# One level of a seven-product scheme in the second product of two MLPs, with weight sums made by DMA

## The chip, the core and the metric

The kernel runs on one core of a Trainium2 chip. The metric is the device time of one execution in microseconds (us); lower is better. The kernel before took 1751.53 us as the median of three runs (1750.19 to 1755.14).

## The reference, cut to what matters

Two transformer blocks run one after the other on x of 512 tokens by 1024 features, all in 32-bit floats. Each block has a mixer and an MLP with a hidden width of 4096; the first has a cross-attention over 256 memory rows between them. The part that is changed:

```python
def squared_relu_mlp(h, w1, w2):                 # first block: ffn_w1 (1024x4096), ffn_w2 (4096x1024)
    return jnp.square(jax.nn.relu(h @ w1)) @ w2
x = x + squared_relu_mlp(rmsnorm(x, norm_ffn[l]), ffn_w1[l], ffn_w2[l])
...
u = rmsnorm_2(x, norm_mlp_g[i]) @ w_up[i]        # second block: w_up_2, w_down_2, same sizes
x = x + jnp.square(jax.nn.relu(u)) @ w_down[i]
```

The first block's mixer (`hybrid_mixer`) holds a gated delta rule with 4 heads. The second block's mixer holds an mLSTM and a sliding-window attention.

## The kernel before, in words

x stays in SBUF with features on the 128 partitions: 8 tiles of 128 features by 512 tokens. A product with a weight is computed in three matmuls: both operands are split into a high part (a cast to float32r) and a low part (the rest, again float32r), and high*high, high*low and low*high are added in one PSUM bank (`mm3`, lines 227 to 229). A *granule* is 256 output features of a weight over 1024 inputs. It comes as two loads of 512 KB by SP's queue into `wr` (line 207, two buffers); ScalarE casts each to `wh` (line 210) and VectorE subtracts to get `wl` (line 211). Then TensorE does two output tiles with 8 x 3 = 24 matmuls of 512 columns each (`proj_fm`).

`ffn` cuts the hidden width into 4 quarters of 1024. `up(q)` makes one quarter of the hidden layer: VectorE takes max(.,0) times the token's norm from PSUM (line 805), ScalarE squares (806), and the result is split into high and low (256, 257). `down(q)` multiplies that quarter with 1024 rows of the second weight and adds the tiles into x (line 402). The order written is up 0, up 1, down 0, up 2, down 1, up 3, down 2, down 3; two sets of slots hold two quarters at a time.

The order on each engine's queue is not written out by hand: the framework records the operations with their dependencies and a scheduler puts each at a place in its engine's queue by estimated times. An operation whose inputs are there early can so be put far ahead of its place in the program text. On the chip every engine works through its queue in that fixed order; an instruction that waits holds all behind it on that engine. DMAs are issued by instructions in the queues of SP, ScalarE (ACT) and GpSimd (POOL), and a wait ahead of a DMA sits in that queue too.

The first mixer (0 to about 308 us) does projections, and for each of the 4 heads `dn_head`: GpSimd makes `slg` from a mask and the decay (line 536), TensorE multiplies it (513), ScalarE takes the exponential (539), GpSimd masks it (540), and all later steps of the head need it: VectorE makes `dM` from it (547), GpSimd masks that (568), and so on. GpSimd also scales the gating values (373, 374), gates each head's output (669) and adds squares for the norms (271).

## Time and profile before

| | |
|---|---|
| runs shown, median | 1751.53 us |
| the profiled execution's own time | 1754.69 us |
| its span, first to last instruction | 1752.9 us |
| TensorE busy / weight loads busy | 1722.4 us (98%) / 1431.2 us (82%) |
| VectorE / ScalarE / GpSimd busy | 1010.4 us (58%) / 722.1 us (41%) / 144.0 us (8%) |
| moved by DMA | 155.09 MB, 88 GB/s on average |
| first MLP, first to last product | about 458 to 818 us |

"Busy" is the time in which the profile shows an instruction on the engine. Matmuls are pipelined, so the time from one matmul's start to the next's is read from the timeline, not from the length shown for one. Idle time of an engine that nobody waits for costs nothing. "DMA share" is the mean busy share of the core's 16 DMA engines.

### The profile page before, as it was taken

The page shows a single profiled execution, that of the slowest core. Times are in us where ns is not written, and L with a number is a line of the kernel's source. Part 1 is how long each engine was busy: PE and PEld are TensorE (multiplying, and loading weights), DVE is VectorE, ACT ScalarE, POOL GpSimd, SP SyncE. Part 2 cuts the span into 40 slices and gives each one's busy share as a digit, 9 for nine tenths or more (in the row PEclk, how much of TensorE's full clock was granted, in tenths as well). Part 3 has the DMA queues.
Part 4 walks back from the last instruction along what each step waited for, and adds up shares of the span by engine and source line. Part 5 has one row for each costly group of instructions (what it writes and reads, how often), then busy time and mean ns, then how long its engine had stood idle before and what let it go on. Part 6 is the DMA issues. An engine that isn't in the chain of part 4 may idle for free.

```text
span 1752.9 us, 22699 instructions
## 1 busy us (share of the span) xinstructions
PE 1722.4 (98%) x8772; PEld 1431.2 (82%) x8772; DVE 1010.4 (58%) x2037; ACT 722.1 (41%) x1258; POOL 144.0 (8%) x123
## 2 busy tenths in 40 slices
PE   8999999999999999999999999999999999999998
PEld 7987788878888888888888887788888888888887
DVE  6998886655544434447756469865555434344455
ACT  5344544544432333334444447654234323232344
POOL 2212311201000000012000000000120000000101
PEclk9999998999999999999999999999999999999999
DMA  6322232312322223222222221223232223233221
GB/s 197 97 73 63 62 98 87 108 49 73 96 97 96 96 96 96 91 91 85 73 73 81 88 73 49 73 72 97 87 97 88 91 95 97 96 96 108 90 99 64
DMA packets 49676, 155.09 MB, mean 88 GB/s; under 512 B 9504, under 2 KB 10656, under 8 KB 49568
## 3 DMA queue, kind: packets, MB, share of 16 engines
q1 hardware_dynamic: 48848, 152.51, 27.3%
q8 instruction: 69, 1.13, 0.3%
q10 hardware_dynamic: 720, 1.13, 0.2%
q14 instruction: 39, 0.32, 0.1%
HBM read 151.26 MB, written 2.10 MB: 87 GB/s over the span
## 4 chain that ended last, share of the span: by engine, by line
PE 87%; DVE 9%; ACT 2%; issue 1%; DMA 0%; POOL 0%; SPq 0%; ACTq 0%; DVEq 0%
PE psd L228 26%; PE psd L229 26%; PE psd L227 25%; DVE wl L211 2%; PE c L564 1%; ACT wh L210 1%; PE c L513 1%; PE lg L1148 1%; PE po L1175 1%; DVE e L314 1%; PE m L1069 1%; DVE S L369 1%; PE c L229 0%; PE c L228 0%; PE c L227 0%
## 5 line engine op out<-in xcount | busy, mean ns | idle before, releaser
L229 PE MATMUL psd<-S,wl 128*128 128x512 f32 (+1 forms) x1936 | 759.4, 392 | 0.5 <-DVE wl L211 0.5
L227 PE MATMUL psd<-S,wh 128*128 128x512 f32 (+1 forms) x1936 | 757.0, 391 | 0.0
L228 PE MATMUL psd<-S,wh 128*128 128x512 f32 (+1 forms) x1872 | 735.0, 393 | 0.0
L211 DVE TENSOR_TENSOR wl<-wr,wh 128x1024 fp32r<-128x1024 f32 (+2 forms) x284 | 351.0, 1236 | 229.9 <-ACT wh L210 228.8
L210 ACT CAST wh<-wr 128x1024 fp32r<-128x1024 f32 (+2 forms) x284 | 292.5, 1030 | 436.5 <-PE psd L228 406.4
L227 PEld LDWEIGHTS psd<-S,wh 128*128 128x128 f32 x1936 | 365.9, 189 | 79.1 <-ACT S L256 0.4
L229 PEld LDWEIGHTS psd<-S,wl 128*128 128x128 f32 x1936 | 364.7, 188 | 76.7 <-DVE wl L211 1.1
L228 PEld LDWEIGHTS psd<-S,wh 128*128 128x128 f32 x1872 | 352.4, 188 | 74.6 <-DVE S L260 0.5
L271 POOL TENSOR_TENSOR acc<-acc,sq 128x512 f32<-128x512 f32 (+1 forms) x47 | 67.7, 1439 | 918.6 <-ACT sq L269 918.4
L402 DVE TENSOR_TENSOR x_fm<-psd,x_fm 128x512 f32<-128x512 f32 x88 | 60.7, 690 | 137.9 <-PE psd L229 137.8
L228 PE MATMUL psd<-wl,S 128*128 128x256 f32 (+2 forms) x480 | 137.5, 286 | 0.6 <-DVE wl L211 0.6
L229 PE MATMUL psd<-wh,S 128*128 128x256 f32 (+2 forms) x480 | 137.1, 286 | 0.0
L227 PE MATMUL psd<-wh,S 128*128 128x256 f32 (+2 forms) x480 | 136.7, 285 | 0.0
L805 DVE SCALAR_TENSOR_TENSOR e<-psd,bc 128x512 f32<-128x512 f32 x64 | 44.3, 692 | 112.3 <-PE psd L229 109.4
L806 ACT ACTIVATE e<-e 128x512 f32<-128x512 f32 x64 | 40.5, 633 | 135.1 <-DVE e L805 135.1
L228 PEld LDWEIGHTS psd<-wl,S 128*128 128x128 f32 x480 | 91.7, 191 | 1.4 <-DVE wl L211 1.0
L227 PEld LDWEIGHTS psd<-wh,S 128*128 128x128 f32 x480 | 91.8, 191 | 0.4
L229 PEld LDWEIGHTS psd<-wh,S 128*128 128x128 f32 x480 | 91.9, 191 | 0.1
L257 DVE TENSOR_TENSOR S<-e,S 128x512 fp32r<-128x512 f32 (+1 forms) x84 | 56.7, 675 | 49.3 <-ACT S L256 49.2
L256 ACT CAST S<-e 128x512 fp32r<-128x512 f32 (+1 forms) x84 | 50.5, 601 | 42.9 <-POOL e L932 27.1
L259 ACT ACTIVATE S<-x_fm,vec 128x512 fp32r<-128x512 f32 x40 | 28.9, 722 | 56.8 <-DVE x_fm L402 37.4
L314 DVE SCALAR_TENSOR_TENSOR e<-e,vec,e 128x511 f32<-128x511 f32 (+2 forms) x60 | 46.6, 779 | 2.6 <-ACT e L311 2.2
(418 smaller groups left out, 1523.0 us busy)
## 6 DMA issues: line engine op xcount, KB each, us to landing
wr<-in_ffn_w_dram SPq DMA_DIRECT2D x64, 512.0 KB
wr<-in_w_up_dram SPq DMA_DIRECT2D x32, 512.0 KB
wr<-in_w_down_dram SPq DMA_DIRECT2D x32, 512.0 KB
wr<-in_w_in_qk_dram SPq DMA_DIRECT2D x16, 512.0 KB
wr<-in_w_in_v_dram SPq DMA_DIRECT2D x12, 512.0 KB
wr<-in_xa_wk_dram SPq DMA_DIRECT2D x8, 512.0 KB
wr<-in_xa_wv_dram SPq DMA_DIRECT2D x8, 512.0 KB
wr<-in_xa_wq_dram SPq DMA_DIRECT2D x8, 512.0 KB
```

The costliest lines, as they stand in the source:

```text
L210: nc.scalar.copy(hi[:, c], raw[:, c])
L211: nc.vector.tensor_tensor(out=lo[:, c], in0=raw[:, c], in1=hi[:, c].bitcast(F32), op=ALU.subtract)
L227: mm(ps, ah, bh, start=first, stop=False)
L228: mm(ps, ah, bl, start=False, stop=False)
L229: mm(ps, al, bh, start=False, stop=last)
L256: nc.scalar.copy(hi, src)
L257: nc.vector.tensor_tensor(out=lo, in0=src, in1=hi.bitcast(F32), op=ALU.subtract)
L271: eng.tensor_tensor(out=acc, in0=acc, in1=sq, op=ALU.add)
L314: nc.vector.scalar_tensor_tensor(out=c[:, s:], in0=xr[:, :T - s], scalar=w(j), in1=c[:, s:], op0=ALU.mult, op1=ALU.add)
L402: self.nc.vector.tensor_tensor(out=self.x[:, o], in0=ps, in1=self.x[:, o], op=ALU.add)
L805: nc.vector.scalar_tensor_tensor(out=t, in0=ps, scalar=0.0, in1=bc, op0=ALU.max, op1=ALU.mult)
L806: nc.scalar.activation(t, t, AF.Square)
```

## The change

**The scheme.** In each MLP, for each quarter q and each granule of 256 outputs, the second product is 256 outputs x 1024 inputs times 1024 inputs x 512 tokens. The outputs, the inputs and the tokens are each cut into two halves. Instead of eight products of halves seven are done, of sums of halves (Strassen's scheme in Winograd's form). `st_gemm` does per granule 7 products of 4 x 3 = 12 matmuls with 256 columns, 84 in all, in place of 48 with 512 columns, and adds each finished PSUM value into a 128x256 part of x, 7 additions per granule; four of the seven products go on adding in a PSUM tile that has just been read (`more=True`).

**The operands of the hidden layer.** `st_fill` makes, per up granule, four sums and differences of halves (`ms`) on VectorE, and splits all seven operand parts into high and low. There is one set of slots; the order is now up 0, down 0, up 1, down 1, and so on.

**The weights.** The second weights are laid out so that one granule is four pieces of 128x512 per partition block (`halves`). Three of the seven weight operands are such pieces, four are sums of them. The sums stand in DRAM tiles, 1 MB for each of the 16 granules of each MLP. `sum_jobs` makes them with DMAs from DRAM to DRAM: per granule three copies issued on ScalarE's queue (4 pieces of 256 KB in all), then four DMAs on GpSimd's queue that add 256 KB each to what stands at the destination (`accum_op`); the third waits for the first, the fourth for the third. The program text calls one step of these jobs before each granule load (`job`): the first MLP's from the first mixer on, the second's from the first MLP on. `st_weights` then loads 7 pieces per granule (three loads of 512 KB, one of 256 KB), where two loads of 512 KB were before, and splits them. In the MLPs the loads rotate over five sets of buffers in place of two `wr` and three `wh`, `wl`.

**Slots.** To make room, slots are renumbered (`perm`), the pool `sp2`/`sp3` is dropped in the MLPs for `fp`, four PSUM banks go to `px`, the input `p` of the last stage is loaded ahead of the second MLP, and the work after the last addition into an x tile (`post`) is called for two tiles at the end of a granule.

**Order on GpSimd.** First head of the first mixer, GpSimd's queue. Before, between the scaling of the gating values (lines 373, 374) and the first head's masks:

```order
L373 TENSOR_TENSOR S_42_322<-S_42_322,S_41_321 128x256
L374 TENSOR_TENSOR S_42_322<-S_42_322,S_41_321 128x256
L536 TENSOR_TENSOR slg_1238<-masks,dg_1052 128x512
L540 TENSOR_TENSOR slg_1238<-slg_1238,masks 128x512
L568 TENSOR_TENSOR dT_1273<-dM_1258,masks 128x512
L536 TENSOR_TENSOR slg_1600<-masks,dg_1052 128x512
```

Now, from the last adding DMAs of the first MLP to the first head's second mask (line 584 was 536, 588 was 540, 616 was 568); the bracket names what the instruction waits for, where DMASW and DMAHW are completions of earlier DMAs from GpSimd and from SP or ScalarE:

```order
L584 TENSOR_TENSOR slg_1307<-masks,dg_1114 128x512 [waits DVE_49]
L219 DMA sums_ffn_w_14_77<-sums_ffn_w_14_77 128x512 [waits DMAHW5_49,DMASW0_49]
L219 DMA sums_ffn_w_15_78<-in_ffn_w_dram 128x512 [waits DMAHW2_49]
L219 DMA sums_ffn_w_14_77<-sums_ffn_w_14_77 128x512 [waits DMASW4_49,DMASW2_49]
L219 DMA sums_ffn_w_15_78<-in_ffn_w_dram 128x512 [waits DMAHW3_49]
...
L219 DMA sums_w_down_1_80<-in_w_down_dram 128x512 [waits DMAHW3_49]
L588 TENSOR_TENSOR slg_1307<-slg_1307,masks 128x512 [waits Activation_49]
L219 DMA sums_w_down_1_80<-sums_w_down_1_80 128x512 [waits DMASW7_49,DMASW5_49]
```

All 128 adding DMAs, those of the second MLP (`sums_w_down`) too, now stand in the first mixer's part of the queue: 58 ahead of the first head's first mask, 71 ahead of its second, and all 128 ahead of the last head's second mask (the fourth `L588`). Behind it no such DMA follows.

**Order on ScalarE.** Near the start of the first mixer, where the weights `w_in_gv` are cast (line 256 was 210). Before:

```order
L210 CAST wh_336<-wr_335 128x1024
L210 CAST wh_342<-wr_341 128x1024
L210 CAST wh_508<-wr_507 128x1024
```

Now:

```order
L256 CAST wh_373<-wr_372 128x1024 [waits DMAHW4_49,DVE_49,PE_49]
L216 DMA sums_ffn_w_1_64<-in_ffn_w_dram 256x1x512 [waits DMAHW2_49]
L256 CAST wh_379<-wr_378 128x1024 [waits DMAHW5_49,DVE_49,PE_49]
L217 DMA sums_ffn_w_1_64<-in_ffn_w_dram 128x512
L218 DMA sums_ffn_w_1_64<-in_ffn_w_dram 128x512
L216 DMA sums_ffn_w_2_65<-in_ffn_w_dram 256x1x512 [waits DMAHW7_49]
L217 DMA sums_ffn_w_2_65<-in_ffn_w_dram 128x512 [waits DMAHW0_49]
L218 DMA sums_ffn_w_2_65<-in_ffn_w_dram 128x512 [waits DMAHW1_49]
L256 CAST wh_550<-wr_549 128x1024 [waits DMAHW3_49,DVE_49,PE_49]
```

All 96 copies, those of the second MLP too, stand in the first mixer's part of ScalarE's queue; most wait for an earlier DMA. (The number in a bracket's name is no time.)

**Order on TensorE.** From the first MLP's first quarter of `up` to its `down` (`x_5077` and `x_5078` are PSUM tiles of the first granule, `psd_5079` its third; `S_...` the operand's parts). The scheduler does the first 9 matmuls of a product, leaves the last 3, which need the newest up tile, and goes on with another product:

```order
L277 MATMUL x_5078<-S_824_4772,wl_5061 128x256
L275 MATMUL psd_5079<-S_828_4776,whx_5054 128x256
...
L276 MATMUL psd_5079<-S_829_4777,whx_5054 128x256 [waits DVE_49]
L275 MATMUL x_5077<-S_826_4774,wh_5060 128x256 [waits DVE_49]
...
L277 MATMUL psd_5079<-S_828_4776,wlx_5055 128x256
L275 MATMUL x_5195<-S_830_4778,whx_5172 128x256
L276 MATMUL x_5195<-S_830_4778,whx_5172 128x256
L275 MATMUL x_5078<-S_824_4772,wh_5060 128x256 [waits Activation_49]
```

So 30 matmuls with 256 columns stand between the last `up` matmul and the first that needs the second half of the newest tile in its split form. In the kernel before a whole `up` quarter stood there.

The diff, cut to its core:

```diff
     def slot(self, i, shape, dt=F32):
+        i = self.perm[i]
         return (self.sp if i < 9 else self.sp2).tile(shape, dt, tag=f"S{i}", name=self.uid(f"S{i}"))
...
+    def sum_jobs(self, name):
+        nc, n = self.nc, 16
+        def step(i):
+            if i < n:
+                a, s = self.D[name][i], self.sums[name][i]
+                nc.scalar.dma_start(s[:, 1::2], a[:, 0:2])
+                nc.scalar.dma_start(s[:, 0:1], a[:, 2:3])
+                nc.scalar.dma_start(s[:, 2:3], a[:, 2:3])
+            acc = lambda o, i: nc.gpsimd.dma_start(o, i, accum_op=ALU.add)
+            if 0 <= i - 1 < n:
+                a, s = self.D[name][i - 1], self.sums[name][i - 1]
+                acc(s[:, 0:1], a[:, 3:4])
+                acc(s[:, 2:3], a[:, 0:1])
+            if 0 <= i - 2 < n:
+                s = self.sums[name][i - 2]
+                acc(s[:, 1:2], s[:, 0:1])
+            if 0 <= i - 3 < n:
+                s = self.sums[name][i - 3]
+                acc(s[:, 3:4], s[:, 1:2])
+        self.jobs += [(lambda i=i: step(i)) for i in range(n + 3)]
+    def job(self):
+        if self.jobs:
+            self.jobs.pop(0)()
+    def wtiles(self, kt, n):
+        p, b, x = self.wp, (2, 3), ""
+        if self.wx is not None:
+            self.wn = (self.wn + 1) % 5
+            if self.wn > 2:
+                p, b, x = self.wx, (2, 2), "x"
+        return (self.t(p, [P, kt, n], "wr" + x, bufs=b[0]), self.t(p, [P, kt, n], "wh" + x, F32R, bufs=b[1]),
+                self.t(p, [P, kt, n], "wl" + x, F32R, bufs=b[1]))
...
         nc = self.nc
-        raw = self.t(self.wp, [P, kt, n], "wr", bufs=2)
-        hi = self.t(self.wp, [P, kt, n], "wh", F32R)
-        lo = self.t(self.wp, [P, kt, n], "wl", F32R)
+        raw, hi, lo = self.wtiles(kt, n)
...
     def wgran(self, name, g, n=256, nk=8, pieces=None):
+        if self.wx is None:
+            self.job()
...
-    def mm3(self, ps, ah, al, bh, bl, first, last):
+    def mm3(self, ps, ah, al, bh, bl, first, last, more=False):
         mm = self.nc.tensor.matmul
-        mm(ps, ah, bh, start=first, stop=False)
-        mm(ps, ah, bl, start=False, stop=False)
-        mm(ps, al, bh, start=False, stop=last)
+        mm(ps, ah, bh, start=first, stop=False, skip_group_check=more)
...
-    def ffn(self, w1, w2, xh, xl, acc, evac):
...
-        rs = self.tok_rs(acc, "rs")
-        bc = self.tok_bc(rs, "bc")
-        H = {}
...
-        up(0)
-        up(1)
-        down(0, self.add_res)
-        up(2)
-        down(1, self.add_res)
-        up(3)
-        down(2, self.add_res)
-        down(3, evac)
...
+        ms = self.t(self.fp, [P, 4, 256], "ms", bufs=1)
+        TT(out=ms[:, 3], in0=e2[:, h[1]], in1=e1[:, h[1]], op=ALU.subtract)
+        TT(out=ms[:, 1], in0=e1[:, h[0]], in1=e1[:, h[1]], op=ALU.subtract)
+        STT(out=ms[:, 2], in0=ms[:, 3], scalar=-1.0, in1=e1[:, h[0]], op0=ALU.mult, op1=ALU.subtract)
+        STT(out=ms[:, 0], in0=ms[:, 2], scalar=-1.0, in1=e2[:, h[0]], op0=ALU.mult, op1=ALU.subtract)
+        self.split_sb(t[6][:, 0, k], t[6][:, 1, k], e1[:, h[0]])
+        self.split_sb(t[4][:, :, k], t[5][:, :, k], e2.rearrange("p (a c) -> p a c", a=2))
+        self.split_sb(t[2][:, :, k], t[3][:, :, k], ms[:, 2:4])
+        self.split_sb(t[0][:, :, k], t[1][:, :, k], ms[:, 0:2])
+    def st_weights(self, name, g):
+        a, s = self.D[name][g], self.sums[name][g]
+        out = []
+        for src in (a[:, 0:2], s[:, 0:2], s[:, 2:4], a[:, 3:4]):
+            hi, lo = self.wload(src, src.shape[1], T)
+            out.extend((hi[:, i], lo[:, i]) for i in range(src.shape[1]))
+        return [out[i] for i in (0, 2, 3, 1, 4, 5, 6)]
...
+    def st_gemm(self, name, g, H, o1, post):
+        nc = self.nc
+        TT = nc.vector.tensor_tensor
+        w = self.st_weights(name, g)
+        _, hi, lo = H
+        X, Z = (self.t(self.px, [P, T], "x")[:, :256] for _ in range(2))
+        Y = self.psd()[:, :256]
+        x = [[self.x[:, o1 + n, t * 256:t * 256 + 256] for t in range(2)] for n in range(2)]
+        def prod(i, ps, m, first):
+            ah, al = w[i]
+            for k in range(4):
+                c = slice(k * P, (k + 1) * P)
+                self.mm3(ps, ah[:, c], al[:, c], hi[m][:, k], lo[m][:, k], first and k == 0, k == 3, not first)
+        def add(n, t, ps, op=ALU.add):
+            TT(out=x[n][t], in0=x[n][t], in1=ps, op=op)
+        prod(0, X, 0, True)
+        add(0, 0, X)
+        prod(1, Z, 4, True)
+        add(1, 1, Z, ALU.subtract)
+        prod(2, X, 5, False)
+        add(0, 1, X)
+        prod(3, Y, 1, True)
+        add(0, 0, Y)
+        prod(4, X, 6, False)
+        add(1, 1, X, ALU.subtract)
+        prod(5, Z, 2, False)
+        add(0, 1, Z)
+        prod(6, X, 3, False)
+        add(1, 0, X, ALU.subtract)
+        for o in (o1, o1 + 1):
+            post(o)
+    def ffn(self, w1, w2, xh, xl, acc, slots, post):
+        nc = self.nc
+        with self.tc.tile_pool(name=self.uid("px"), bufs=4, space=PSUM) as self.px:
+            bc = None
+            for q in range(4):
+                H = None
+                for g in range(4):
+                    pss, es = [], []
+                    self.proj_fm(self.wgran(w1, 4 * q + g), xh, xl, (0, 1), lambda o, ps: pss.append(ps))
+                    self.job()
+                    if bc is None:
+                        bc = self.tok_bc(self.tok_rs(acc, "rs"), "bc")
+                    for ps in pss:
+                        e = self.t(self.fp, [P, T], "eh", bufs=4)
+                        nc.vector.scalar_tensor_tensor(out=e, in0=ps, scalar=0.0, in1=bc, op0=ALU.max, op1=ALU.mult)
+                        nc.scalar.activation(e, e, AF.Square)
+                        es.append(e)
+                    H = H or self.st_operand(slots)
+                    self.st_fill(H, g, *es)
+                for g in range(4):
+                    self.st_gemm(w2, 4 * q + g, H, 2 * g, post if q == 3 else lambda o: None)
...
         K = Kern(tc, ctx, D, out, dbg)
         K.setup()
+        K.sum_jobs("ffn_w2")
         K.mixer()
         mem = K.memory()
         with tc.tile_pool(name="sp2", bufs=1) as K.sp2:
             op = K.w_out1()
             op = K.xattn(*op, mem)
+        K.sum_jobs("w_down_2")
+        with tc.tile_pool(name="fp", bufs=1) as K.fp:
+            K.sp2 = K.wx = K.fp
             ev, fin = K.between()
-            K.ffn("ffn_w1", "ffn_w2", *op, ev)
+            K.ffn("ffn_w1", "ffn_w2", *op, (0, 1, 4, 7, 8, 9, 10), ev)
+            K.wx = None
             op2 = fin()
+        K.perm = [2, 3, 5, 6, 0, 1, 4, 7, 8]
         mh, ml = K.mixer2(*op2)
-        with tc.tile_pool(name="sp3", bufs=1) as K.sp2:
-            xh, xl = K.pair((9, 10)), K.pair((11, 12))
-            acc = K.new_acc()
-            def ev(o, ps):
-                K.nc.vector.scalar_tensor_tensor(out=K.x[:, o], in0=ps, scalar=0.5, in1=K.x[:, o], op0=ALU.mult, op1=ALU.add)
-                K.norm_tile(o, xh, xl, acc, "norm_mlp_g_2")
-            for g in range(4):
-                K.proj_fm(K.wgran("w_out_2", g), mh, ml, (2 * g, 2 * g + 1), ev)
-            K.dump("x5", K.x)
+        K.perm = list(range(13))
...
+def halves(w):
+    v = w.reshape(4, 2, P, -1, 2, P).transpose(3, 2, 4, 1, 0, 5).reshape(-1, P, 4, 4 * P)
+    return np.ascontiguousarray(v)
```

86 lines of the change are left out of this document (50 added, 36 removed).

## The prediction, made before the changed kernel was run

> **What bounds the kernel now.** I read the page's first part and its chain first.
>
> ```profile
> PE 1722.4 (98%) x8772; PEld 1431.2 (82%) x8772; DVE 1010.4 (58%) x2037; ACT 722.1 (41%) x1258; POOL 144.0 (8%) x123
> PE 87%; DVE 9%; ACT 2%; issue 1%; DMA 0%; POOL 0%; SPq 0%; ACTq 0%; DVEq 0%
> PE psd L228 26%; PE psd L229 26%; PE psd L227 25%; DVE wl L211 2%; PE c L564 1%; ACT wh L210 1%; PE c L513 1%; PE lg L1148 1%; PE po L1175 1%; DVE e L314 1%; PE m L1069 1%; DVE S L369 1%; PE c L229 0%; PE c L228 0%; PE c L227 0%
> ```
>
> TensorE's product matmuls are 77% of the chain; no DMA and no GpSimd work is on it. Next the busy times by stretch, for the first mixer (to about 308 us) and one stretch of the first MLP. Columns: stretch, its length, busy us of PE, PEld, DVE, ACT, POOL with their counts, clock, DMA share, GB/s.
>
> ```profile
> 0.00:44.00 44.00, 38.95 (x215) 33.74 (x216) 28.91 (x53) 24.40 (x40) 11.22 (x16) 1.00 0.60 196
> 44.00:88.00 44.00, 43.46 (x302) 39.94 (x302) 40.34 (x112) 16.80 (x25) 12.50 (x16) 1.00 0.31 97
> 88.00:132.00 44.00, 42.59 (x258) 36.89 (x257) 40.10 (x84) 20.94 (x52) 7.16 (x5) 1.00 0.22 73
> 132.00:176.00 44.00, 42.94 (x249) 34.99 (x248) 39.36 (x115) 17.43 (x42) 9.04 (x8) 1.00 0.20 63
> 176.00:220.00 44.00, 41.20 (x235) 33.93 (x234) 36.58 (x93) 22.71 (x64) 14.14 (x14) 0.92 0.22 63
> 220.00:264.00 44.00, 40.95 (x340) 38.84 (x339) 38.81 (x145) 21.06 (x54) 7.47 (x4) 1.00 0.33 97
> 264.00:308.00 44.00, 40.68 (x298) 38.78 (x297) 27.40 (x69) 18.30 (x41) 4.80 (x3) 0.88 0.32 95
> 458.00:548.00 90.00, 90.00 (x389) 1.00 0.29 94
> ```
>
> In the MLP TensorE has no gap at all, so fewer columns there are time won. The mixer is another case: TensorE is at 92 to 99% and VectorE, until 264 us, at 83 to 92%; the heads' chains run through GpSimd, and TensorE's gaps from 44 to 308 us are only 264 - 251.8 = 12 us. A head that comes late has little to hide behind.
>
> **The products.** The start of one matmul after another, 512 and 256 columns, from the timeline:
>
> ```profile
> 620.18 0.40 PE L227 MATMUL psd<-S,wh 128*128 128x512 f32 x1
> 631.32 0.39 PE L227 MATMUL psd<-S,wh 128*128 128x512 f32 x1
> 885.04 0.28 PE L227 MATMUL psd<-wh,S 128*128 128x256 f32 x1
> 889.94 0.28 PE L227 MATMUL psd<-wh,S 128*128 128x256 f32 x1
> ```
>
> 48 matmuls lie in the first 11.14 us (0.2321 each), 42 in the second 4.90 us (0.1167 each): half the columns, half the time, so short matmuls lose nothing here. A granule goes from 48 x 0.2321 = 11.14 to 84 x 0.1167 = 9.80 us; 32 granules win 42.8 us.
>
> What lies beside it in the MLP:
>
> ```profile
> L211 DVE TENSOR_TENSOR wl<-wr,wh 128x1024 fp32r<-128x1024 f32 x266 | 333.5, 1254 | 227.9 <-ACT wh L210 226.9
> L257 DVE TENSOR_TENSOR S<-e,S 128x512 fp32r<-128x512 f32 x76 | 53.4, 702 | 49.1 <-ACT S L256 49.1
> L256 ACT CAST S<-e 128x512 fp32r<-128x512 f32 x76 | 47.2, 621 | 35.2 <-POOL e L932 27.1 <-DVE e L395 6.2
> L805 DVE SCALAR_TENSOR_TENSOR e<-psd,bc 128x512 f32<-128x512 f32 x64 | 44.3, 692 | 112.3 <-PE psd L229 109.4 <-ACT bc L293 2.9
> L806 ACT ACTIVATE e<-e 128x512 f32<-128x512 f32 x64 | 40.5, 633 | 135.1 <-DVE e L805 135.1
> L710 DVE TENSOR_TENSOR e<-psd,bc x8: 404/419/425, 232.5 to 266.6; 128x256 f32<-128x256 f32 x8
> ```
>
> VectorE per up granule: two weight subtracts 2.5, two line-805 operations 1.4, four `ms` at 0.42 each 1.7, splits 0.42 + 3 x 0.70 = 2.5, together 8.1 of 11.1 us; per down granule 3.5 subtracts 4.4 and seven additions 2.9, together 7.3 of 9.8 us. That is 74%, where TensorE is full: hidden. Loads grow from 2.10 to 2.88 MB per pair of granules in 20.9 us, 138 GB/s at a share of about 0.43: hidden. From up to down the newest tile needs 0.69 + 0.63 + 0.62 + 0.70 = 2.6 us, 3.9 with one weight subtract ahead of it on VectorE, and TensorE has 30 x 0.1167 = 3.5 us of other matmuls; I take 1 us for each of 8 transitions, 8 us (nothing, up to 8 x 5.8 = 46 if no cover held and all `ms` and splits showed). The late `post` for two tiles costs about 3 us per MLP, 6 us. The MLPs together: -42.8 + 8 + 6 = **-29 us**.
>
> **The sums.** They are the other half of the matter. 32 granules x 4 pieces of 256 KiB are 33.55 MB copied and as much added, and the order puts all of it into the first mixer. What a DMA engine gives, from loads with the same 2 KB rows:
>
> ```profile
> x_fm<-in_x_dram SPq DMA_DIRECT2D x8, 256.0 KB
> wr<-in_w_in_u_dram SPq DMA_DIRECT2D x8, 256.0 KB
> 4.00:8.00 4.00, 3.30 (x15) 2.75 (x15) 1.91 (x6) 2.62 (x5) 0.00 (x0) 1.00 0.95 296
> 24.00:28.00 4.00, 4.00 (x19) 3.29 (x18) 1.21 (x1) 2.04 (x2) 0.33 (x1) 1.00 0.92 331
> ```
>
> 296 GB/s at 0.95 is 312 GB/s at full share (360 in the second row, with longer rows). One pass over 33.55 MB takes 107.5 us of all 16 engines. The trace has no DMA from DRAM to DRAM and no adding one, so I bound them. From below: copy and addition cost one pass each, 215 us. From above: every byte read and written in DRAM is paid, 2 passes for a copy and 3 for an addition, 538 us. I take one for a copy and two for an addition, which has to read its destination as well as its source: 323 us; reads are what the rows above show.
>
> When are they needed? GpSimd's own times:
>
> ```profile
> 51.05 0.74 POOL L373 TENSOR_TENSOR S<-S,S 128x256 f32<-128x256 f32 x1 [21.89 <-DVE S L369]
> 92.79 2.08 POOL L536 TENSOR_TENSOR slg<-masks,dg 128x512 f32<-128x512 f32 x1 [23.73 <-DVE dg L478]
> 230.58 1.88 POOL L540 TENSOR_TENSOR slg<-slg,masks 128x512 f32<-128x512 f32 x1 [11.25 <-ACT slg L539]
> 0.74 0.38 SPq L162 DMA_DIRECT2D x_fm<-in_x_dram  x1
> 1.65 0.42 SPq L162 DMA_DIRECT2D x_fm<-in_x_dram  x1
> ```
>
> 58 adding DMAs have to be issued before the instruction of 92.79 us, all 128 before that of 230.58 us, and most wait in GpSimd's queue until an earlier one has landed. By TensorE's order the last head comes about 4 us later now, so the sums may take until 235 us. They start at about 20 us. The kernel's own loads up to there need 0.60 x 24 + (0.31 + 0.22 + 0.20 + 0.22) x 44 + 0.33 x 15 = 61 us of the engines. So the sums end at 20 + 61 + 323 = 404 us, 169 us late; TensorE's gaps take 12 us of that: **+157 us**. (One pass: 296 us, net +49. Both sides paid: 619, net +372.) Behind the waiting DMAs stand the masks of all four heads; TensorE, in fixed order, waits at line 513's product for them, and VectorE at `dM`.
>
> Issue costs: 96 copies on ScalarE at 0.42 us are 40 us beside 17 to 23 us of work in 44; 128 DMAs on GpSimd at 0.42 us are 54 us, at its slowest instruction above (2.08 us) 266 us, no more than the wait already priced. Both lie inside it; without it ScalarE's 40 us would show at the casts.
>
> "Collectives: The Full Stack" of the Trainium skill says, in its passage on why ReduceScatter is half of AllGather, that an addition inside the DMA engine costs no extra cycles but two source reads on the same ring, so half the throughput of a copy. No run here shows it; by that rule the sum stays as it is.
>
> **The sum.** Against the profiled execution's 1754.7 us (span 1752.9 and 1.8 around it): 1754.7 - 29 + 157 = 1882.7. The median of the runs lies 3.2 us lower than that execution: **1880 us**.
>
> **Rivals.** *The sums are hidden*: the DMAs keep up with the mixer, and only the MLPs' gain is left: 1754.7 - 29 - 3.2 = 1722 us. For it: the share is only 0.20 to 0.33 there, and no DMA is on the chain. Against: between 20 and 235 us the engines have 215 - 61 = 154 us free and one pass over both halves already needs 215. It decides if DRAM to DRAM moves over 67.1/154 us = 436 GB/s, which no row shows. *Additions cost one pass*: net +49, 1772 us. *Both sides are paid*: each piece is written to DRAM as well as read, in a 16-engine stream that the trace only knows with SBUF at one end; net +372, 2095 us; for it, every addition also waits for the one before to land. "DMA: Bandwidth & Descriptors" of the Trainium skill gives, under "Latency and other measured facts", 207 to 214 GB/s for copies between DRAM tensors; an estimate by it (160 us for the copies, 320 for the additions) ends the sums at 561 us and gives 2036 us. No run here shows it yet. *The scheme wins nothing* because 84 weight loads of 0.19 us would not hide: against it stand the 0.1167 us starts, which include such loads; under 0.03, part of the rest.
>
> **The numbers.** About 0.3%, 5 us, is what a measurement of this kernel can tell from no change. Chances: two passes 0.42 (1880), one pass 0.20 (1772), both sides 0.15 (2095), hidden 0.18 (1722), the rest 0.05, split between within 0.3% (it needs net +24 to +34 us) and either side. Faster 0.19, same 0.04, slower 0.77. The range is 1722 to 2060: it takes in one and two passes and the lower half of "both sides", and leaves out the lower half of "hidden". The forecast's own range, with the rate between 280 and 360 GB/s, is 1830 to 1920.
>
> **What would show it.** Right: the DMA share over 0.9 from 20 us until about 400 us; the adding DMAs' queue ending there; GpSimd's first `slg` mask at about 200 instead of 93 us, and TensorE idle in the mixer waiting on GpSimd or `slg`; in the MLPs 256-column starts 0.117 us apart, each MLP some 14 us shorter. Wrong: the last adding DMA issued by 235 us, or a mixer that ends at 308 us. A first MLP that is longer than before would mean that the additions or the up-to-down change are on the path.

## The result, and the profile after

The changed kernel is slower: 2022.83 us as the median of four runs (2021.1 to 2026.91) against 1753.28 us (1750.19 to 1755.14), a ratio of 1.1543 with a 95% interval of 1.1516 to 1.1569. The direction and the place were as forecast and the time lies inside the stated range of 1722 to 2060, but outside the forecast's own range of 1830 to 1920: the loss is 270 us where 128 were forecast. One of the six runs of the kernel with own PSUM tiles, further below, took 2735.98 us at a granted clock of 0.555; that kernel's ratio leaves this run out, its median of 1728.22 us does not (1726.73 us without it).

The page of the changed kernel, its first part, its chain of waits and its three large DMA queues. In a queue's row stand its packets, its MB and the share of 16 engines' span that its packets took; q1 is SP's queue, q10 ScalarE's, q0 GpSimd's.

```profile
PE 1746.6 (87%) x9924; PEld 1508.3 (75%) x9924; DVE 1181.5 (59%) x2453; ACT 800.9 (40%) x1388; POOL 246.2 (12%) x251
PE 65%; DMA 17%; DVE 6%; issue 6%; ACT 3%; POOL 2%; SPq 0%; ACTq 0%; DVEq 0%; POOLq 0%
q1 hardware_dynamic: 58064, 177.68, 27.8%
q0 software_dynamic: 18432, 33.56, 12.9%
q10 hardware_dynamic: 18640, 34.69, 6.1%
```

A sixth of the chain is now DMA, where it was 0%. TensorE is busy for 24 us more than before and the span is 266 us longer, so TensorE stands still for 242 us more. Where it stands the stretches of the changed kernel show (length, busy us of PE, PEld, DVE, ACT, POOL with counts, clock, DMA share, GB/s):

```profile
44.00:88.00 44.00, 35.52 (x258) 34.98 (x259) 17.79 (x71) 13.76 (x21) 9.05 (x11) 0.82 1.02 220
88.00:132.00 44.00, 17.71 (x57) 12.82 (x55) 14.53 (x40) 8.91 (x14) 12.91 (x17) 0.68 0.95 210
...
220.00:264.00 44.00, 12.20 (x53) 10.11 (x53) 6.01 (x20) 4.90 (x13) 12.64 (x15) 0.62 0.90 126
264.00:308.00 44.00, 8.80 (x32) 7.73 (x33) 5.89 (x9) 1.39 (x6) 16.48 (x19) 0.54 0.76 100
...
440.00:484.00 44.00, 24.81 (x144) 21.46 (x142) 16.08 (x41) 14.77 (x49) 15.41 (x20) 0.73 0.75 142
484.00:528.00 44.00, 32.74 (x218) 30.98 (x218) 33.50 (x125) 13.26 (x36) 15.15 (x14) 0.84 0.42 82
```

The DMA engines are busy for 0.75 to 1.02 of the time until about 484 us, and TensorE is busy for a fifth to four fifths of it. GpSimd's timeline of the changed kernel, at the first head's first and second mask (lines 584 and 588) and at the last adding DMA and the last head's second mask:

```profile
241.08 1.97 POOL L584 TENSOR_TENSOR slg<-masks,dg 128x512 f32<-128x512 f32 x1
...
288.53 1.87 POOL L588 TENSOR_TENSOR slg<-slg,masks 128x512 f32<-128x512 f32 x1
...
500.88 0.81 POOL L219 DMA_DIRECT2D sums_w_down<-sums_w_down  x1
510.46 1.26 POOL L588 TENSOR_TENSOR slg<-slg,masks 128x512 f32<-128x512 f32 x1 [8.76 <-ACT slg L587]
```

The last of these stood at 230.58 us before, so it comes 279.9 us later. The waits of the first 620 us say what held GpSimd, and what TensorE waited for (engine and line that wait, what they wait for, us in all, times, longest):

```profile
POOL sums_ffn_w L219 <- DMA sums_ffn_w<-sums_ffn_w: 96.9, 15, 10.4
POOL sums_ffn_w L219 <- DMA sums_ffn_w<-in_ffn_w_dram: 75.4, 17, 12.7
POOL sums_w_down L219 <- DMA sums_w_down<-in_w_down_dram: 69.2, 19, 6.4
POOL sums_w_down L219 <- DMA sums_w_down<-sums_w_down: 65.8, 12, 10.1
PE c L561 <- POOL slg L584: 55.0, 1, 55.0
```

GpSimd stood 307 us at adding DMAs until an earlier DMA had landed, and TensorE stood 55 us at one stroke until the first mask came.

For all kernels below I cut the profiled execution at four places: the start of the last addition into x at the end of the first mixer, at the end of the cross-attention and at the end of the second mixer, and the last instruction. Before and after, the first of these is

```profile
331.13 0.69 DVE L402 TENSOR_TENSOR x_fm<-psd,x_fm 128x512 f32<-128x512 f32 x1 [0.56 <-PE psd L229]
```

```profile
611.22 0.69 DVE L450 TENSOR_TENSOR x_fm<-psd,x_fm 128x512 f32<-128x512 f32 x1 [0.56 <-PE psd L277]
```

| us | first mixer | cross-attention | first MLP and second mixer | second MLP and end | span |
|---|---|---|---|---|---|
| before | 331.1 | 118.1 | 872.7 | 431.0 | 1752.9 |
| after | 611.2 | 117.7 | 868.0 | 422.3 | 2019.2 |
| difference | +280.1 | -0.4 | -4.7 | -8.7 | +266.3 |

TensorE in the first mixer, before and after:

```profile
0.00:331.00 331.00, 313.74 (x1985) 275.55 (x1986) 268.22 (x685) 156.08 (x336) 74.90 (x72) 0.97 0.32 99
```

```profile
0.00:611.00 611.00, 366.62 (x1984) 320.01 (x1985) 259.05 (x685) 156.02 (x338) 175.15 (x200) 0.76 0.79 164
```

It stands still for 227 us more there. The other 53 us are busy time: the same matmuls take longer, at a granted clock of 0.76 in place of 0.97. How much of this lies on the path is not shown.

So two things are to be explained: 280 us in the first mixer where 157 were forecast, and a gain of 13 us in the MLPs where 29 were.

### The profile page after: what moved, and what is told of

It reads as the page before. It is cut to its first block, busy times and chain, and to the rows that moved or that the text cites. A ratio compares the mean times of both kernels' runs of the same rounds, so it can differ in the third digit from the quotient of the medians.

```text
span 2019.2 us, 26176 instructions
## 1 busy us (share of the span) xinstructions
PE 1746.6 (87%) x9924; PEld 1508.3 (75%) x9924; DVE 1181.5 (59%) x2453; ACT 800.9 (40%) x1388; POOL 246.2 (12%) x251
## 3 DMA queue, kind: packets, MB, share of 16 engines
q0 software_dynamic: 18432, 33.56, 12.9%
## 4 chain that ended last, share of the span: by engine, by line
PE 65%; DMA 17%; DVE 6%; issue 6%; ACT 3%; POOL 2%; SPq 0%; ACTq 0%; DVEq 0%; POOLq 0%
PE psd L276 16%; PE psd L275 16%; PE psd L277 16%; DMA sums_ffn_w<-in_ffn_w_dram 5%; DMA sums_w_down<-in_w_down_dram 4%; PE x L275 4%; PE x L276 3%; PE x L277 3%; DMA sums_ffn_w<-sums_ffn_w 2%; DVE wl L257 2%; ACT wh L256 1%; PE c L612 1%; DMA dY<-dV 1%; POOL sums_ffn_w L219 1%; DMA sums_w_down<-sums_w_down 1%
## 5 line engine op out<-in xcount | busy, mean ns | idle before, releaser
L277 PE MATMUL psd<-S,wl 128*128 128x512 f32 (+1 forms) x1256 | 492.8, 393 | 9.5 <-DVE wl L257 9.5
L275 PE MATMUL psd<-S,wh 128*128 128x512 f32 (+1 forms) x1256 | 492.4, 393 | 7.6 <-ACT wh L256 4.7
L276 PE MATMUL psd<-S,wh 128*128 128x512 f32 (+1 forms) x1192 | 467.4, 392 | 1.7 <-DVE S L308 1.7
L257 DVE TENSOR_TENSOR wl<-wr,wh 128x1024 fp32r<-128x1024 f32 (+1 forms) x266 | 321.9, 1211 | 182.5 <-ACT wh L256 180.3
L256 ACT CAST wh<-wr 128x1024 fp32r<-128x1024 f32 (+1 forms) x266 | 266.1, 1001 | 340.3 <-PE psd L276 174.7
L277 PEld LDWEIGHTS psd<-S,wl 128*128 128x128 f32 x1256 | 242.4, 193 | 57.3 <-DVE wl L257 11.4
L275 PEld LDWEIGHTS psd<-S,wh 128*128 128x128 f32 x1256 | 243.3, 194 | 54.8 <-ACT wh L256 5.9
L276 PEld LDWEIGHTS psd<-S,wh 128*128 128x128 f32 x1192 | 231.0, 194 | 45.5 <-DVE S L308 1.9
L275 PE MATMUL x<-S,wh 128*128 128x256 f32 x452 | 130.5, 289 | 7.5 <-DVE x_fm L892 7.4
L276 PE MATMUL x<-S,wh 128*128 128x256 f32 x452 | 127.4, 283 | 0.0
L277 PE MATMUL x<-S,wl 128*128 128x256 f32 x452 | 126.4, 282 | 0.0
L276 PE MATMUL psd<-S,whx 128*128 128x512 f32 (+1 forms) x296 | 108.8, 367 | 0.6 <-DVE S L305 0.6
L275 PE MATMUL psd<-S,whx 128*128 128x512 f32 (+1 forms) x296 | 108.0, 366 | 0.0
L277 PE MATMUL psd<-S,wlx 128*128 128x512 f32 (+1 forms) x296 | 107.1, 362 | 0.0
```

What stands on the lines that cost most here:

```text
L256: nc.scalar.copy(hi[:, c], raw[:, c])
L257: nc.vector.tensor_tensor(out=lo[:, c], in0=raw[:, c], in1=hi[:, c].bitcast(F32), op=ALU.subtract)
L275: mm(ps, ah, bh, start=first, stop=False, skip_group_check=more)
L276: mm(ps, ah, bl, start=False, stop=False, skip_group_check=more)
L277: mm(ps, al, bh, start=False, stop=last, skip_group_check=more)
```

## Experiments: what the sums cost

**Nothing, copies alone, plain copies, no chain.** Four kernels, each with one edit of `sum_jobs` (and, in the first, of `st_weights`):

```diff
e1_no_sums
-        self.jobs += [(lambda i=i: step(i)) for i in range(n + 3)]
-        a, s = self.D[name][g], self.sums[name][g]
+        a = s = self.D[name][g]
e2_copies_only
-            acc = lambda o, i: nc.gpsimd.dma_start(o, i, accum_op=ALU.add)
+            acc = lambda o, i: None
e3_plain_copies
+            acc = lambda o, i: nc.gpsimd.dma_start(o, i)
e4_unchained
-                acc(s[:, 1:2], s[:, 0:1])
+                acc(s[:, 1:2], a[:, 2:3])
-                acc(s[:, 3:4], s[:, 1:2])
+                acc(s[:, 3:4], a[:, 0:1])
```

> No copying and no adding DMA at all; the places of the sums are loaded from the plain weights, in the same sizes, so the output is not the reference's. What is left is the rest of the change: seven products, their operands, the larger loads. The prediction's step for the MLPs (-29 us) gives 1753 - 29 = 1724 us. Read from the trace of the changed kernel, where the two MLPs are only some 14 us shorter together, it gives 1739. If the mixer's delay were not from the sums, it stays near 2020.

> The 96 copies stay where they are on ScalarE's queue, the 128 adding DMAs are left out (the output is not the reference's). Theory A (the 16 DMA engines have too much to move): copies took 6.1% of 2019 us = 123 us of the engines, own loads 61 us up to 235 us, start 20: they end at about 204, in time, so 1739 to 1750 us. Theory B (GpSimd stands behind adding DMAs that wait for one another to land): also 1739 to 1750. Rival C (the copies in ScalarE's queue, which wait for earlier copies, hold up the casts): over 1800.

> The 128 DMAs on GpSimd's queue keep their place, their waits and their bytes, but copy instead of adding (the output is not the reference's). Theory A: their time on the engines falls from 12.9% of 2019 = 260 us to that of the copies, about 118 us; the sums then end about 140 us sooner and the time is about 1880. Theory B with a landing that takes as long for a copy as for an addition (8 us): 2000 to 2020, no gain.

> The third and fourth adding DMA of a granule take a plain piece as their source in place of the sum just made, so no adding DMA waits for another one of its granule, only for the copies and for the one eight before it (the output is not the reference's). Same number, bytes and place. Theory A: same time, 2000 to 2030. Theory B: GpSimd's 163 us of waits at the adding DMAs whose source is a sum go away, 1860 to 1900.

A fifth kernel joins the edits of the last two.

> Both edits together: the 128 DMAs on GpSimd's queue copy instead of adding, and none reads what another has just written (the output is not the reference's). Place and bytes as in the change. What is left is the engines' throughput for two passes of copying: 126 us (the copies alone) and 143 us (plain copies from GpSimd's queue) and 61 us of own loads, from 20 us on: end at 350, 115 us later than needed, so about 1748 + 115 = 1863. If serial waits were a fixed loss for each DMA on GpSimd's queue, as slow as plain copies with the chain: 1930.

| | us | ratio to before, 95% interval | first mixer, us |
|---|---|---|---|
| without sums (e1) | 1747.94 | 0.9969 (0.9944 to 0.9995) | 337.4 |
| copies only (e2) | 1769.49 | 1.0104 (1.0070 to 1.0139) | 360.6 |
| plain, unchained (e7) | 1853.46 | 1.0561 (1.0534 to 1.0588) | 442.8 |
| adding, unchained (e4) | 1927.17 | 1.1005 (1.0972 to 1.1037) | 520.7 |
| plain, chained (e3) | 1931.54 | 1.1032 (1.1005 to 1.1060) | 513.9 |
| adding, chained (the change) | 2022.83 | 1.1543 (1.1516 to 1.1569) | 611.2 |

Without sums the mixer's loss is gone but for 6 us, so nearly all of it comes from them. The copies alone, forecast as nearly free or over 1800 us, cost 23 us of the mixer against the kernel without sums: the last is issued at 235.7 us, and ScalarE stands at them for 16 us in four waits. The two kernels with one edit each (e3, e4) fall between their two theories, the one with both (e7) 10 us under its 1863. To them the 128 DMAs on GpSimd's queue add 82 us if they only copy and none reads what another has just written; adding in place of copying costs another 78, the chain another 71, both together 168. What an adding DMA costs the engines shows in the row of GpSimd's queue. Plain copies with the chain (e3) and without (e7), then additions without the chain (e4):

```profile
q0 software_dynamic: 10240, 33.56, 7.4%
```

```profile
q0 software_dynamic: 10240, 33.56, 6.6%
```

```profile
q0 software_dynamic: 18432, 33.56, 11.4%
```

For the same 33.56 MB that is 7.4% of a span of 1926.0 = 143 us, 6.6% of 1851.8 = 122 us and 11.4% of 1931.3 = 220 us; in the change it is 12.9% of 2019.2 = 260 us. So an addition took 1.8 times as long as a plain copy, with the chain and without. An adding DMA of 256 KB also goes as 144 packets in place of 80. The chain's cost is of another kind. The stretch from 88 to 132 us of the two kernels with plain copies, in the chain (e3) and without it (e7):

```profile
88.00:132.00 44.00, 16.79 (x72) 13.76 (x71) 12.14 (x22) 6.20 (x8) 18.79 (x31) 0.66 0.75 191
```

```profile
88.00:132.00 44.00, 27.83 (x130) 22.82 (x129) 27.09 (x50) 12.52 (x19) 13.39 (x23) 0.82 1.00 295
```

Without the chain the engines are full (1.00); with it they stand for a quarter of this stretch, where GpSimd waits for one landing after another. So both theories hold a half: the bytes (theory A) and the serial waits (theory B) each cost 70 to 80 us, and together more than the sum of the two alone.

**Half the sums.**

```diff
-        K.sum_jobs("w_down_2")
...
+        a = s = self.D[name][g]
+        if name == "ffn_w2":
+            s = self.sums[name][g]
```

> The change with half the sums: those of the first MLP are made as before, those of the second are left out and plain weights loaded in their place (the output is not the reference's). By the prediction's step (the mixer is late by what the sums end after 235 us; 64 additions end at about 270 us): 1748 + 35 = 1783. By the order on GpSimd's queue (58 of these 64 additions stand ahead of the first head's first mask, which then comes at 241 us in place of 93, and the four heads follow from there as before): 1748 + 149 to 175 = 1900 to 1920, so half the bytes cost well over half of the loss.

1891.05 us, ratio 1.0769 (1.0733 to 1.0805), first mixer 474.1 us: near the 1900 to 1920 read from the order, far from 1783. All four second masks in one row (min, median, max, then first and last start):

```profile
L588 POOL TENSOR_TENSOR slg<-slg,masks x4: 1401/1503/1874, 258.1 to 373.6; 128x512 f32<-128x512 f32 x4
```

The adding DMAs whose source is a sum, in the same form:

```profile
L219 POOL DMA_DIRECT2D sums_ffn_w<-sums_ffn_w x32: 807/814/1730, 36.3 to 257.6; - x32
```

Before the change the four ran from 113.1 to 230.6 us. With half the sums the first is 145 us late and the last 143: the heads follow one another as they always did, from where the first was let go. Half of the bytes cost 143 of 280 us, though the last of these additions is issued at 257.6 us, only 27 us after the last mask stood before. So it matters what stands ahead of the first head, and not only when the last addition is done. The other 64 additions, between the heads' masks, cost the other 137.

## Experiments: the sums elsewhere

**Held back by a gate.** A granule's copies must wait for four words of x, written to the sums' tile first; the sums of the first MLP so come behind the first mixer and those of the second in the first MLP, where two steps are called per weight granule. The second kernel also moves the adding of squares for the norms of that stage from GpSimd to VectorE.

```diff
                 a, s = self.D[name][i], self.sums[name][i]
+                nc.gpsimd.dma_start(s[0:1, :, 0:1], self.x[0:1, 0:4, 0:1])
...
             op = K.w_out1()
+            K.sum_jobs("ffn_w2")
e6_gated_dve
+            eng = nc.gpsimd if k < KT - 1 and not self.jobs else nc.vector
```

> The whole change with its true sums, but each granule's copies have to wait for four words of x that are written after the first mixer: the sums of the first MLP so lie behind the mixer (from about 335 us), those of the second in the first MLP. No DMA is left out. Theory (the 270 us come from where the sums stand, in front of the heads' masks on GpSimd, and not from the bytes as such): 33.55 MB copied and added now lie beside work that wants no GpSimd, so the time is that of the kernel without sums, 1748, up to 1765 where additions to the norms wait on GpSimd behind adding DMAs. Rival (the bytes cost wherever they stand, since loads for TensorE come late beside them): 380 us of the engines' time are still to be paid, over 1850.

> As the gated kernel, and the adding of squares for the norm behind the cross-attention is done by VectorE in place of GpSimd, so that nothing of TensorE's path stands behind an adding DMA. Theory of place: 1740 to 1750, as the kernel without sums (1748), and up to 15 us less than the gated one if the norms were held up there. Rival (the bytes cost wherever they stand): as much as the gated one.

1902.49 us (1.0834, 1.0800 to 1.0867) and 1894.20 us (1.0779, 1.0753 to 1.0804): over 1850, as the rival had it, but largely for another reason. The first mixer is back at 331.9 us in the second of them, but the stretch from the first MLP through the second mixer takes 999.7 us in place of 868.0. ScalarE's timeline there, at the first copies for the second MLP:

```profile
560.95 1.05 ACT L257 CAST wh<-wr 128x1024 fp32r<-128x1024 f32 x1 [0.89 <-PE x L277]
611.43 0.57 ACTq L217 DMA_DIRECT2D sums_w_down<-in_w_down_dram  x1
612.12 1.04 ACT L257 CAST whx<-wrx 128x1024 fp32r<-128x1024 f32 x1 [50.12 <-DMA sums_w_down<-x_fm]
```

The copy waited for its gate, the gate stood in GpSimd's queue behind additions, and the casts of the weights stood behind the copy for 50 us. The wait had only changed its queue.

**Nothing else in the queue, then spread out.** Next the copies too are issued by GpSimd, and all that GpSimd computed behind the first mixer is done by VectorE. The second kernel of the pair also paces the sums: each granule's gate is a copy of four words by ScalarE from a weight of the running work.

```diff
e9_gated_pool
-                nc.scalar.dma_start(s[:, 1::2], a[:, 0:2])
+                nc.gpsimd.dma_start(s[:, 1::2], a[:, 0:2])
...
-        nc.gpsimd.tensor_tensor(out=E, in0=E, in1=self.maskb("upper"), op=ALU.mult)
+        nc.vector.tensor_tensor(out=E, in0=E, in1=self.maskb("upper"), op=ALU.mult)
e13_paced
+            self.nc.scalar.copy(tok, hi[0:1, 0, 0:4].bitcast(F32))
+            self.jobs.pop(0)(tok)
```

> As the gated kernel with norms on VectorE, but the copies too are issued on GpSimd's queue, and everything that GpSimd computed behind the first mixer is done by VectorE; the sums of the second MLP may run on into the second mixer. So the sums are the only work of GpSimd from about 320 us on, and no queue that TensorE needs holds a DMA of them that waits. No DMA is left out. In the gated kernels ScalarE stood up to 50 us at a copy that waited for its gate, with the casts behind it. Theory (the loss is what stands in a queue behind a waiting DMA): 1745 to 1760. Rival (the engines are so full beside the MLP that its own loads come late): 1800 or more.

> As the kernel in which only GpSimd carries the sums, but each granule's copies wait for a small copy that ScalarE makes from a weight granule of the running work: one granule of sums per weight granule in the cross-attention, one per two in the first MLP (each 22 us), the second MLP's mostly in the second mixer. Same DMAs, spread out. A granule of sums is 384/32 = 12 us of the engines. If bursts were the matter: the 22 us that the first MLP lost go away, 1748 to 1757. If the bytes cost wherever they stand: 1770 to 1780 again.

1775.03 us (1.0116, 1.0079 to 1.0152) and 1769.74 us (1.0078, 1.0049 to 1.0106). So 119 of the 137 us that the second gated kernel still lost against before went with this edit, which frees the shared queues and also lets the second MLP's sums run on into the second mixer. Pacing gave little: the two intervals overlap, as the rival had it (1770 to 1780). In the profiled runs it took the first MLP and second mixer from 903.0 to 888.7 us, where the kernel without sums takes 870.3; the other three parts lie within about 3 us of that kernel's. The first MLP, to its last addition into x, of the paced kernel and then of the one without sums:

```profile
455.30:834.60 379.30, 354.18 (x2135) 315.84 (x2134) 243.07 (x402) 159.28 (x230) 81.77 (x117) 0.96 0.82 197
```

```profile
455.30:808.60 353.30, 345.58 (x2129) 307.72 (x2128) 239.75 (x389) 157.30 (x214) 16.20 (x13) 1.00 0.40 126
```

The paced kernel's first MLP is 26 us longer: TensorE is busy 9 us more, at a clock of 0.96, and stands for 17 us more. With a DMA share of 0.82 ScalarE's casts wait 33.6 us for loads of first-MLP weights where they waited 15.5, and TensorE waits 22.0 us for VectorE's additions into x where it waited 7.5. That the late loads are the cause is argued from these figures, not shown by an edit; VectorE also does GpSimd's work there. In the second mixer, where the paced sums raise the share to 0.56, no loss is seen: it takes 510 us against 517.

**Sums in SBUF by GpSimd.** No DMA from DRAM to DRAM: the four pieces are loaded once and GpSimd adds. In the second kernel VectorE's weight subtractions for these are made piece by piece.

```diff
+        TT = nc.gpsimd.tensor_tensor
+        TT(out=sa[:, 0], in0=r23[:, 0], in1=r23[:, 1], op=ALU.add)
+        TT(out=sa[:, 1], in0=r01[:, 0], in1=sa[:, 0], op=ALU.add)
+        TT(out=r23[:, 0], in0=r23[:, 0], in1=r01[:, 0], op=ALU.add)
+        TT(out=r01[:, 1], in0=r01[:, 1], in1=sa[:, 1], op=ALU.add)
e11_fine
+            for i in range(hi.shape[1]):
+                nc.vector.tensor_tensor(out=lo[:, i], in0=raw[:, i], in1=hi[:, i].bitcast(F32), op=ALU.subtract)
```

> The whole change with true sums, but no DMA from DRAM to DRAM: in each MLP granule the four pieces are loaded once and GpSimd makes the four sums of 128x512 in SBUF with four additions. GpSimd's additions of this size took 1.3 to 2.1 us, so 5 to 8 us per granule of 9.8 us, on an engine that is idle there; loads fall from 1.75 to 1 MB per granule. If the rest of the MLP is as in the kernel without sums (1748): 1740 to 1750, a version that costs nothing in the mixer. Rival: VectorE, at over 70% in the MLPs, is slowed by GpSimd's additions beside it, or the sums come late for their casts: over 1760.

> As the kernel with GpSimd's sums in SBUF, and VectorE's weight subtractions for them are done piece by piece (0.68 us) in place of two pieces at once (1.23 us). Own PSUM tiles for the products won 20 us, so waits for VectorE's additions are worth up to that. If an addition is late because it stands behind one long subtraction: 5 to 10 us less than without this edit. If VectorE is late as a whole: the same or up to 5 us more, since two short operations take 0.13 us longer than a long one.

1825.41 us (1.0394, 1.0373 to 1.0415) and 1805.45 us (1.0286, 1.0262 to 1.0310): the rival was right. The mixer lost nothing (336.3 us), but the MLPs did. In the first kernel's first MLP VectorE is busy 273 us with 388 operations, where it took 240 us for 389 without sums; the stage up to the end of the second mixer is 37 us longer. ScalarE's casts also wait there for GpSimd's sums, 25.7 us in four waits, so both halves of the rival have a part. Two groups of VectorE's in the first MLP, the split of `ms` with both inputs in SBUF and the addition into x with one input in PSUM, with GpSimd's sums (e10) and without sums (e1), mean ns behind the comma:

```profile
L309 DVE TENSOR_TENSOR S<-ms,S 128x512 fp32r<-128x512 f32 x32 | 28.4, 915 | 2.3 <-ACT S L308 2.3
L913 DVE TENSOR_TENSOR x_fm<-x_fm,x 128x256 f32<-128x256 f32 x93 | 37.7, 416 | 26.5 <-PE x L281 25.9
```

```profile
L304 DVE TENSOR_TENSOR S<-ms,S 128x512 fp32r<-128x512 f32 x30 | 19.7, 688 | 2.6 <-ACT S L303 2.5
L891 DVE TENSOR_TENSOR x_fm<-x_fm,x 128x256 f32<-128x256 f32 x96 | 39.2, 416 | 25.0 <-PE x L276 25.0
```

The first took 915 ns in place of 688, the second 416 in both. "SBUF — State Buffer" of the Trainium skill says under "Who interferes with whom" that a VectorE instruction with two SBUF inputs and a GpSimd instruction that reads SBUF lock each other out, and that one with a single SBUF input does not (outside the two-port modes); the two rows agree with it. Why shorter subtractions gave 20 us here and nothing in the kernels below is open.

## Experiments: what the MLPs lost

**Own PSUM tiles.** Without sums, each product starts a PSUM tile of its own.

```diff
-            self.mm3(ps, ..., first and k == 0, k == 3, not first)
+            ps = self.t(self.px, [P, T], "x")[:, :256]
+            self.mm3(ps, ..., k == 0, k == 3)
```

> The kernel without sums (1748 us), and each of the seven products goes into a PSUM tile of its own in place of adding to a tile that VectorE has just read (the output is not the reference's). The MLPs gained 8 us there in place of the 29 predicted. If the rest is lost where a product has to wait until VectorE has read the tile it adds to (about 9 us of waits in the first MLP, 6 in the second, and some 50 starts of 0.09 us in each): 1735 to 1740. If VectorE is simply too full in the MLPs: 1748, as without this edit.

The median is 1728.22 us, ratio 0.9834 (0.9811 to 0.9857), 20 us less than without sums. By the medians it is 29 us faster than the kernel before (1757.16 in that comparison). In the profiled run, the fastest of this kernel, first MLP and second mixer take 857.1 us, second MLP and end 412.7: 15.6 and 18.3 us less than before, together 34. So the seven products do win what they should, 29 us or somewhat more; the step that lost it was the addition to a tile that has just been read. TensorE's waits for such additions in the first MLP, in the changed kernel and then with own tiles:

```profile
PE x L275 <- DVE x_fm L892: 8.0, 7, 2.4
```

```profile
PE x L274 <- DVE x_fm L892: 2.0, 2, 1.5
```

The changed kernel's VectorE and then its TensorE at one of these places:

```profile
814.97 1.23 DVE L257 TENSOR_TENSOR wl<-wr,wh 128x1024 fp32r<-128x1024 f32 x1 [1.26 <-ACT wh L256]
816.11 0.74 DVE L892 TENSOR_TENSOR x_fm<-x_fm,x 128x256 f32<-128x256 f32 x2
```

```profile
815.13 0.28 PE L277 MATMUL x<-S,wlx 128*128 128x256 f32 x1
816.67 0.36 PE L275 MATMUL x<-S,whx 128*128 128x256 f32 x1 [1.26 <-DVE x_fm L892]
```

The addition of 0.41 us stands behind a subtraction that had itself waited for its cast, and TensorE starts 1.42 us late. Beside some 9 us of such gaps in the first MLP, 58 steps from one matmul to the next in such tiles take 0.16 to 0.30 us and not 0.117; with own tiles it is 4 steps.

**Shorter subtractions, or fewer.** Three more kernels: pieces of 128x512 without sums, the same in the paced kernel, and (in the kernel of the next section) three of seven low parts by GpSimd.

```diff
+            st = max(1, 512 // n) if self.wx is not None else kt
+            for i in range(c.start, c.stop, st):
e17_second_pool
+            (eng or nc.vector).tensor_tensor(out=lo[:, c], ..., op=ALU.subtract)
```

> The kernel without sums (1748 us; the output is not the reference's) with the weight subtractions in pieces of 128x512 in the MLPs, nothing else. Additions late behind long subtractions: 1733 to 1740, near the 1728 of own PSUM tiles. VectorE late as a whole: 1748 to 1753.

> The paced kernel, and in the MLPs VectorE makes each low part of a weight in pieces of 128x512 (0.68 us) in place of 128x1024 (1.23 us), so that an addition waits behind a shorter operation. With GpSimd's sums in SBUF this edit gave 20 us. If it gives 10 to 15 here and pacing works: 1733 to 1747, faster than the kernel before (1757 in that comparison, 1753 in all). If VectorE is late as a whole: no less than the paced kernel.

> As the kernel with the seven products in the second MLP alone, and three of the seven weight parts of a granule get their low part from GpSimd in place of VectorE, which so has 2.0 us less of its 7.3 us in a down granule of 9.8; GpSimd has nothing else there. If VectorE is late because it is too full: the second MLP's waits for additions (about 6 to 10 us) go away, 5 to 10 us less than without this edit, 1734 to 1740. If GpSimd's slower operations (3 us for 128x1024 by its 1.3 us for 128x512) make the low parts late: no less, or more.

1747.27 us (0.9946, 0.9923 to 0.9969), 1774.11 us (1.0094, 1.0059 to 1.0128) and 1752.65 us (0.9982, 0.9964 to 0.9999): the first two are no faster than without the edit, and the last is 13 us slower. So one long subtraction ahead of the addition is not the cause by itself. With GpSimd beside it, one of VectorE's operations with two SBUF inputs took 1310 ns where it takes 419 in the kernel of the next section (e17, then e16):

```profile
L862 DVE TENSOR_TENSOR ms<-eh,eh 128x256 f32<-128x256 f32 x16 | 21.0, 1310 | 5.3 <-ACT eh L933 5.3
```

```profile
L862 DVE TENSOR_TENSOR ms<-eh,eh 128x256 f32<-128x256 f32 x16 | 6.7, 419 | 0.0
```

What would take the waits away while the scheme's additions in PSUM are kept is open.

## A version that beats both

In the paced kernel the sums cost nothing where they lay in the second mixer, and the second MLP gained more than the first. So the seven products stay in the second MLP alone; the first MLP is the old one. The sums of the second are paced through the second mixer on GpSimd's queue, which does nothing else there.

```diff
             ev, fin = K.between()
-            K.ffn("ffn_w1", "ffn_w2", *op, (0, 1, 4, 7, 8, 9, 10), ev)
+            K.ffn_plain("ffn_w1", "ffn_w2", *op, ev)
+            K.sum_jobs("w_down_2")
```

> The seven products in the second MLP alone; the first MLP is that of the kernel before. Only the second MLP's sums are made, by GpSimd's queue behind the first MLP, one granule per two weight granules of the second mixer (12 us of the engines per some 22 us, beside a share of 0.25 to 0.33), and GpSimd's calculations of that stage are done by VectorE. Nothing is left out. The second MLP and the end took 431 us before and 422 with the change; the second mixer beside paced sums took no longer than without. So 1753 - 9 = 1744, 0.5% faster than before. If the sums cost there what they cost in the first MLP (9 us for half of them or more): 1750 to 1760.

1739.40 us, ratio 0.9913 (0.9887 to 0.9939), where 1744 were expected: faster than both kernels, if by 0.9% only. Its slowest run (1746.20) lies below the fastest of the kernel before (1747.30). First mixer 330.8, cross-attention 118.2, first MLP and second mixer 870.2, second MLP and end 418.0 us. The stretch from the last addition of the first MLP to the end of the second mixer, in this kernel and in the kernel before the change:

```profile
808.30:1319.10 510.80, 507.59 (x2766) 426.11 (x2765) 338.72 (x816) 250.31 (x502) 88.11 (x124) 1.00 0.63 148
```

```profile
807.90:1322.00 514.10, 509.16 (x2770) 426.06 (x2769) 331.69 (x793) 245.86 (x482) 26.30 (x20) 1.00 0.25 78
```

TensorE stands for 3 us of this stage, and stood for 5 before, while the DMA share goes from 0.25 to 0.63: here the sums are hidden. GpSimd's work of the stage went to VectorE in the same edit, so what each did to the 3 us is not separated.

## Why the prediction was right, and where it was wrong

**Right: what happens, and where.** All sums in the first mixer, the DMA engines full, GpSimd's first mask late (241 us; "about 200" was forecast), TensorE waiting for it, "slower" with 0.77. The kernel without sums shows that nothing else of the change costs the mixer much: 337.4 us there against 331.1, a difference that goes with a lower clock (below). That the time lies inside the stated range says little, since that range holds two of the four named cases whole and half of each of the others; 2022.83 us is nearer to "both sides paid" (2095) than to the forecast (1880).

**Wrong: the size of the sums.** The step that failed is the sum "20 + 61 + 323 = 404 us" for their end, and within it two terms. *The price of a pass.* Forecast were one pass of 107.5 us for the copies and two for the additions, 215. Measured are 6.1% of 2019.2 less the 3.5 us that ScalarE's queue had before, 120 us, and 260 us: 380 in place of 323. Without the chain the additions took 220 us, about the two passes forecast; it is additions that wait for one another that were priced too low. *The time in which the engines wait.* Forecast were 20 us at the start. The last addition is issued at 500.88 us and lands at about 506. The stretch up to there:

```profile
0.00:506.00 506.00, 266.67 (x1342) 228.28 (x1342) 183.67 (x472) 108.24 (x236) 154.12 (x187) 0.73 0.89 178
```

A share of 0.89 is 450 us, so the engines stood 56 us; GpSimd waited for landings one after another, which the prediction named among its rivals and gave no price. What is left for own loads is 450 - 380 = 70 us against 61. So 56 + 70 + 380 = 506 in place of 404, 102 us of the missing 123.

**Wrong: the 12 us that TensorE's gaps were to absorb.** Nothing was absorbed: the last mask is 279.9 us late and the mixer's end 280.1. From the last mask to the mixer's end it is 100.8 us, where it was 100.6. The heads are a chain from mask to mask, and the gaps were parts of that chain. This is another 12. Of the last 9, half lie between the last landing and the last mask, which also waits for ScalarE (8.76 us in its row); the other half is that the forecast counted from 235 us, the last mask before the change from 230.58.

**Right for too simple a reason: "as late as the last sum".** The half-sums kernel shows a second bound: 58 additions ahead of the first head make the whole chain of heads late. By the prediction's step alone that kernel would take 1783 us; it takes 1891. In the change the first head's second mask is 175 us late (288.53 against 113.13) and the last head's 280, so there the end of the sums is the later bound.

**The two rules weighed beside the sum.** "DMA: Bandwidth & Descriptors" of the Trainium skill, under "Latency and other measured facts", has 207 to 214 GB/s for copies between DRAM tensors, for tiles of 16 KiB rows at certain row pitches, so not for the contiguous pieces of this case. Here the engines were busy 120 to 126 us for 33.55 MB, 266 to 280 GB/s, so by this trace copies are cheaper. The estimate by that page, 2036 us, came nearest to the result, but by other terms: it had the copies at 160 us and no idle engines. "Collectives: The Full Stack" of the Trainium skill has half the throughput for an addition inside the engine; 220 against 122 us without the chain and 260 against 143 us with it, additions against plain copies from the same queue, are a factor of 1.8 both times, near it.

**Wrong: the MLPs.** The step is "-42.8 + 8 + 6 = -29 us". The products' own gain is real (29 us by the medians with own PSUM tiles, 34 in the profiled run, all else included), and no wait of the 8 us at the change from up to down shows in the trace. Missing is a term that the prediction did not have: four of seven products go on in a tile that VectorE has to read first, and VectorE, at 74% by the prediction and at 68% in the first MLP measured (239.9 of 354.4 us), is "hidden" only on average. It cost some 20 us, so 13 were left in the profiled run of the change, or 8 in that without the sums.

**The rivals.** "Hidden" is out, since the last addition is issued at 500.88 us; "one pass" and "both sides paid" (619 us for the sums' end) lie on either side of the measured 506.

## What to carry to other kernels

A DMA that waits stops everything behind it on the engine that issues it, so transfers that wait for one another belong on a queue that holds nothing else. Here their place among that engine's other work decided more than their bytes: against the kernel without sums the same bytes cost 275 us ahead of the heads and 22 when paced on a queue of their own. An addition between two DRAM tensors was worth two passes of a load (220 us against 107.5), and nearly two and a half where additions waited for one another (260). Where an operation in PSUM goes on in a tile that another engine has just read, look at the waits for the reader, which its mean load (68% here) did not show.
